# Transposing keys and outputs of a chunked RWKV-7 scan in TensorE's transpose mode

## The chip, the cores and the metric

The kernel runs on one core of one Trainium2 chip, in float32 throughout. The metric is the device time of one execution in microseconds (us). In the profile PE is TensorE's matmul, PEld its weight load, DVE VectorE, ACT ScalarE, POOL GpSimd, SP SyncE, whose queue (SPq) issues most of the DMAs.

## The reference

An encoder of two layers reads 1280 tokens of 1024 channels (a prompt of 256 and a sample of 1024). Layer 0 mixes tokens with a bidirectional RWKV-7 recurrence over 16 heads of 64 channels, layer 1 with neighbourhood attention; each is followed by a squared-ReLU MLP. The change lies in the recurrence alone:

```python
def _wkv_scan(r, w, k, v, a, b, reverse):
    def step(S, inp):
        r_t, w_t, k_t, v_t, a_t, b_t = inp
        sa = jnp.einsum('bhvk,bhk->bhv', S, a_t)
        S = S * w_t[:, :, None, :] + sa[..., None] * b_t[:, :, None, :] + v_t[..., None] * k_t[:, :, None, :]
        return S, jnp.einsum('bhvk,bhk->bhv', S, r_t)
    ...
    _, y = lax.scan(step, s0, seq, reverse=reverse)

# in the mixer: both directions, then a group norm per head, gains, and the bonus
for d in range(2):
    ...
    y = y + _wkv_scan(rf, _heads(decay), k_d, vf, -kk, kk * iclr, reverse=(d == 1))
mu = jnp.mean(y, axis=-1, keepdims=True)
var = jnp.mean(jnp.square(y - mu), axis=-1, keepdims=True)
y = ((y - mu) * lax.rsqrt(var + GN_EPS)).reshape(B, T, C) * lnx_g + lnx_b
y = y + (bonus * vf).reshape(B, T, C)
```

## The kernel before, in words

The scan works on chunks of 64 tokens (`L = 64`), so that the recurrence becomes small matrix products. A job (`scan_job`) takes 16 chunks of one pair of heads: the first head of the pair lies in partitions 0 to 63, the second in 64 to 127. Ten jobs follow each other, and each runs both directions, `d` = 0 forwards and 1 backwards. Within a job the chunks come in groups of four, so there are eight (direction, group) pairs to a job, 80 in all.

The helper `pair` (L995) issues one 64x64 product for each head, one instruction with rows and columns 0 to 63, one with 64 to 127 (or crossed, for the outputs `yo` and `zps`). Every such float32 matmul shows as two records in the trace.

For each (direction, group) pair the program does, among others:

- `prod` (tile `aps`) and `kprod` (tile `kps`): products of keys with queries, masked by DVE into `zb` and `zk`;
- `merge1`, `merge2` (tiles `yps`, `qps`): the second half of an inverse `Q` that DVE and the DMA queues prepare for the next job (`q`, `qt`, `qd`, then `qq` and `qx`);
- `ktr` (L950 to L959), once for each of its four chunks: the keys of both kinds, `bk`, are transposed by multiplying with an identity (tile `lps`, one PSUM bank for both heads), and after the fourth chunk ACT copies the bank to `lt`.

The steps of the recurrence (`scan_step`) use these. A step takes the state `S` through `w` (copied by ACT to `up`), through the inverse (copied to `u`), and through `lt` to the next `S` (ACT again, L1041); its output goes to `yo`. PE, ACT and DVE run in the order in which the program states the work, and that order comes from a time which each piece is given by hand (`at`), so the pieces of `ktr` stand between the steps of the two directions. DMAs on SP's queue are placed by the scheduler.

Four PSUM banks (tag `aps`) go round among the tiles `aps`, `yps`, `kps`, `qps`, `lps` and `zps`. After a job `scan_post` normalises its output `y` in two halves of eight chunks; `tr` (L1114 to L1122) transposes each half, again by products with an identity (tile `zps`), ACT copies it to `zt`, and SP's queue stores it to `z_d`.

Of the kernel before, what the change touches and what calls it, by code (L numbers as in the profile page):

```python
# [5 lines left out]
F32 = mybir.dt.float32  # L6
F32R = mybir.dt.float32r
AF = mybir.ActivationFunctionType
ALU = mybir.AluOpType
# [4 lines left out]
P = 128  # L14
# [4 lines left out]
L = 64  # L19
# [32 lines left out]
class Trunk:  # L52
# [733 lines left out]
    def at(self, t, f, level=3):  # L786
        self.todo.append((t, len(self.todo), f, level))
# [6 lines left out]
    def scan_job(self, j):  # L794
        nc = self.nc
# [3 lines left out]
        J = {"ar": {}, "zb": {}, "zk": {}, "lt": {}}  # L799
# [12 lines left out]
        for n, (d, g) in enumerate(order):  # L812
            m, c0 = grp[g]
            t = T0 + 2 * n if j != 1 or n < 4 else -16.1 + 0.45 * (n - 4)
# [99 lines left out]
        for n, (d, g) in enumerate(order):  # L914
            m, c0 = grp[g]

            def merge1(d=d, g=g):
                zb, qx, lo = J["zb"][d, g], J["qx"][d], 32 * d
                yps = self.pt.tile([P, 4, 32], F32, name="yps", tag="aps")
                for c in range(4):  # L920
                    self.pair(lambda e, z: (yps[z, c, :], zb[z, c, 0:64], qx[z, 4 * g + c, :]))
                yt = J["yt", d, g] = self.nxt(self.r_yt[d])
                nc.scalar.copy(yt[:, :, lo:lo + 32], yps)

            def merge2(d=d, g=g):
                Q, yt, hi = J["Q"], J["yt", d, g], 32 - 32 * d
                qps = self.pt.tile([P, 4, 32], F32, name="qps", tag="aps")
                for c in range(4):
                    self.pair(lambda e, z: (qps[z, c, :], yt[z, c, :], Q[z, 4 * g + c, d, hi:hi + 32]))
                nc.scalar.copy(Q[:, 4 * g:4 * g + 4, d, hi:hi + 32], qps)  # L930
            t = 2 * n - 3.992
            at(t + 0.52, merge1)
            at(t + 1.30, merge2)

            def kload(d=d, g=g, m=m, c0=c0):
                bk = J["bk", d, g] = self.rp.tile([P, 4, P], F32, name="bk", tag="bk", bufs=3)
                nc.sync.dma_start(bk, self.bk_d[m, d, :, c0:c0 + 4, :])

            def kprod(c, d=d, g=g):
                bk, ar = J["bk", d, g], J["ar"][d, g]  # L940
                if c == 0:
                    J["pk"] = self.pa.tile([P, 4, P], F32, name="kps", tag="aps")
                ps = J["pk"]
                self.pair(lambda e, z: (ps[z, c, :], bk[z, c, 64:128], ar[z, c, :]))

            def kmask(d=d, g=g, ps=None):
                zk = J["zk"][d, g] = self.rp.tile([P, 4, P], F32, name="zk", tag="zk", bufs=3)
                nc.vector.tensor_tensor(out=zk, in0=J["pk"], in1=self.mask[d].unsqueeze(1).to_broadcast([P, 4, P]), op=ALU.mult)

            def ktr(c, d=d, g=g):  # L950
                bk = J["bk", d, g]
                if c == 0:
                    J["pl"] = self.pt.tile([P, 4, 2, L], F32, name="lps", tag="aps")
                ps = J["pl"]
                for i in range(2):
                    self.pair(lambda e, z: (ps[z, c, i, :], bk[z, c, 64 * i:64 * i + 64], self.ident[z, z]))
                if c == 3:
                    lt = J["lt"][d, g] = self.rp.tile([P, 4, 2, L], F32, name="lt", tag="lt", bufs=3)
                    nc.scalar.copy(lt, ps)  # L959
            at(t - 1.9 if j or n > 1 else -19.0 + 0.1 * n, kload)  # L960
            at(t + 1.25, kmask)
            for c in range(4):
                at(t + c * 0.11 + 0.80, lambda c=c, f=kprod: f(c))
                at(t + c * 0.11 + 1.53, lambda c=c, f=ktr: f(c))
# [17 lines left out]
        st = [{"S": None}, {"S": None}]  # L982
        for d in range(2):
            for i in range(16):
                cc = i if d == 0 else 15 - i
                m, c0 = grp[cc // 4]
# [13 lines left out]
    def scan_step(self, at, t, J, st, d, cc, m, ch, new, end, i, last):  # L1000
        nc = self.nc
        g, c = cc // 4, cc % 4
        R = {}
        w, us, sn = (lambda s=s: self.pbank[d][:, s] for s in (slice(0, L), slice(L, 2 * L), slice(2 * L, 3 * L)))
        yb = lambda: self.ybank[i // 4 % 2]
        yo = lambda: yb()[:, int(g > 1), c, :]
        half = self.half

        def s0():
            zk, vt = J["zk"][d, g], J["vt"]  # L1010
            self.pair(lambda e, z: (w()[z], zk[z, c, 0:64], vt[z, 0, cc, :]))

        def s1():
            ar, zk, vt = J["ar"][d, g], J["zk"][d, g], J["vt"]
            S = R["S"] = None if new else st["S"]
            if S is not None:
                self.pair(lambda e, z: (w()[z], ar[z, c, 0:64], S[z]), start=False, free=True)
            up = R["up"] = self.sp.tile([P, L], F32, name="up", tag="up", bufs=4)
            nc.scalar.copy(up, w())
            self.pair(lambda e, z: (yo()[half(1 - e)], zk[z, c, 64:128], vt[z, 0, cc, :]), start=d == 0 and i % 4 == 0, free=True)  # L1020

        def s2():
            Q, up, S, ar, vt = J["Q"], R["up"], R["S"], J["ar"][d, g], J["vt"]
            if S is not None:
                self.pair(lambda e, z: (yo()[half(1 - e)], ar[z, c, 64:128], S[z]), start=False, free=True)
            if not end:
                lt = J["lt"][d, g]
                self.pair(lambda e, z: (sn()[z], lt[z, c, 1, :], vt[z, 0, cc, :]), start=False, free=True)
                if S is not None:
                    self.pair(lambda e, z: (sn()[z], self.ident[z, z], S[z]), start=False, free=True)  # L1030
            self.pair(lambda e, z: (us()[z], Q[z, cc, d, :], up[z]), start=last, free=True)
            u = R["u"] = self.sp.tile([P, L], F32, name="u", tag="u", bufs=4)
            nc.scalar.copy(u, us())

        def s3():
            u, zb, y = R["u"], J["zb"][d, g], J["y"]
            if not end:
                lt = J["lt"][d, g]
                self.pair(lambda e, z: (sn()[z], lt[z, c, 0, :], u[z]), start=False, free=True)
                S2 = self.sp.tile([P, L], F32, name="S", tag="S", bufs=5)  # L1040
                nc.scalar.activation(S2, sn(), AF.Copy, scale=self.dall[:, m, d, ch:ch + 1])  # L1041
                st["S"] = S2
            self.pair(lambda e, z: (yo()[half(1 - e)], zb[z, c, 64:128], u[z]), start=False, free=True)
            if d == 1 and i % 4 == 3:
                lo = min(g, 3 - g)
                y = y.rearrange("p (x c) v -> p x c v", c=4)[:, lo:4 - lo:3 - 2 * lo]
                if i < 8:
                    nc.vector.tensor_copy(y, yb())
                else:
                    nc.vector.tensor_tensor(out=y, in0=yb(), in1=y, op=ALU.add)  # L1050
        at(t - 0.68, s0)
        at(t, s1)
        at(t + 0.33, s2)
        at(t + 0.66, s3)

    def scan_post(self, at, J, grp, last):

        nc = self.nc
        for half in range(2):
            st = {}  # L1060
# [3 lines left out]
            t0 = (12.5, 17.496)[half]  # L1064
# [27 lines left out]
            def p3a(st=st, runs=runs):  # L1092
                st["vb"] = self.yp.tile([P, 8, L], F32, name="vb", tag="vb", bufs=2)
                for x, m, c0, g in runs:
                    nc.vector.tensor_tensor(out=st["vb"][:, 4 * x:4 * x + 4], in0=J["vt"][:, 1, 4 * g:4 * g + 4],
                                            in1=self.bonus[:, c0:c0 + 4, m:m + 1].to_broadcast([P, 4, L]), op=ALU.mult)

            def p3b(st=st, runs=runs):
                for x, m, c0, g in runs:
# [12 lines left out]
                eng.tensor_tensor(out=yv(), in0=yv(), in1=st["vb"].rearrange("p (x c) v -> p x c v", c=4), op=ALU.add)  # L1112

            def tr(runs=runs):  # L1114
                ps = self.pt.tile([P, 8, L], F32, name="zps", tag="aps")
                for x, m, c0, g in runs:
                    for c in range(4):
                        self.pair(lambda e, z: (ps[self.half(1 - e), 4 * x + c, :], J["y"][z, 4 * g + c, :], self.ident[z, z]))
                zt = self.yp.tile([P, 8, L], F32, name="zt", tag="zt", bufs=1)
                nc.scalar.copy(zt, ps)  # L1120
                for x, m, c0, g in runs:
                    nc.sync.dma_start(self.scr["z_d"][m, :, c0 * L:(c0 + 4) * L], zt[:, 4 * x:4 * x + 4].rearrange("p c t -> p (c t)"))  # L1122
            for dt, f in ((-0.186, p1), (0.474, p2), (-2.0 - 3.5 * half if last else 1.327, p3a), (1.601, p2b), (-1.9 - 3.5 * half if last else 1.982, p3b), (1.843, p2c), (2.252, p3),
                          (3.521, p4), (4.15, p4b), (4.563, p5), ((6.25, 5.809 if last else 7.25)[half], tr)):
                at(t0 + dt, f)
# [966 lines left out]
```

## Time and profile before

| | |
|---|---|
| median of 3 runs | 3987.63 us (3979.55 to 3991.28) |
| the profiled execution | 3978.29 us, of which its span 3976.5 |
| PE busy | 3742.6 us (94% of the span) |
| DVE, ACT, POOL busy | 2371.8, 1686.8, 1686.1 us |
| the scan, 690 to 1370 us of the span | PE busy 577.24 of 680 us, DVE 374.38, ACT 377.45, POOL 153.85 |
| records of the key transposes (`lps<-cst,bk`) and of the output transposes (`zps<-cst,y`) | 2560 and 640 |
| ACT's copies of them (L959, L1120) | 80 and 20 |

A record's duration on PE is its way through the array; records overlap, so what one costs the engine is the distance between starts, not its duration. In the timeline, rows of the same kind that follow closely are merged (x8), and the second column runs from the first start to the last end.

### The profile page before, as it was taken

What the parts mean: (1) busy time and instruction counts of PE and PEld (TensorE: products, weight loads), DVE (VectorE), ACT (ScalarE), POOL (GpSimd) and SP (SyncE); (2) the same over time, 40 slices, a digit from 0 to 9 for tenths busy, and PEclk for the clock granted to TensorE, in tenths of its full rate; (3) what the DMA queues carried; (4) which work ended last, traced back from release to release, by engine and by line L of the source; (5) the groups of instructions that cost most, each with busy time, mean ns of one, the idle gap of its engine ahead of it and who ended that gap; (6) DMA issues with size and microseconds to landing.
All of it is one profiled execution on the core that took longest, in us unless ns stands there. A gap on an engine that the chain in (4) does not pass through costs nothing.

```text
span 3976.5 us, 89848 instructions
## 1 busy us (share of the span) xinstructions
PE 3742.6 (94%) x36484; PEld 3151.9 (79%) x36484; DVE 2371.8 (60%) x4441; ACT 1686.8 (42%) x4128; POOL 1686.1 (42%) x1540
## 2 busy tenths in 40 slices
PE   8988988888888899999999999999989999999999
PEld 5764578787878787888888889887778788888888
DVE  5778743556565446666666682355563656666666
ACT  6776652555555532222222242466563222222222
POOL 4446552112121334555555551244442445555554
PEclk9997899999999899999999999999999999999999
DMA  4226564767664341111111115444555111111111
GB/s 139 73 100 224 200 227 127 180 164 166 150 165 112 117 131 38 40 38 38 43 43 41 39 61 165 112 109 100 114 135 188 48 35 43 40 43 38 41 40 64
DMA packets 460094, 394.83 MB, mean 99 GB/s; under 512 B 268480, under 2 KB 353856, under 8 KB 459680
## 3 DMA queue, kind: packets, MB, share of 16 engines
q1 hardware_dynamic: 425264, 327.73, 29.8%
q10 hardware_dynamic: 34416, 61.35, 4.2%
q8 instruction: 288, 4.72, 0.5%
q14 instruction: 126, 1.03, 0.1%
HBM read 270.50 MB, written 124.44 MB: 99 GB/s over the span
## 4 chain that ended last, share of the span: by engine, by line
PE 73%; DVE 8%; DMA 7%; ACT 5%; issue 4%; POOL 2%; SPq 1%; ACTq 0%; DVEq 0%; POOLq 0%
PE ps L96 13%; PE ps L97 13%; PE ps L98 12%; PE ps L1480 4%; PE ps L1481 4%; PE ps L1482 4%; PE wu L998 4%; PE vps L513 1%; PE aps L998 1%; PE vps L514 1%; PE vps L515 1%; PE kps L998 1%; DVE q L875 1%; PE op L2004 1%; DMA raw<-in_w_no_dram 1%
## 5 line engine op out<-in xcount | busy, mean ns | idle before, releaser
L96 PE MATMUL ps<-ah,whi 128*128 128x512 f32 (+1 forms) x2304 | 842.8, 366 | 3.9 <-ACT whi L90 3.2
L98 PE MATMUL ps<-ah,wlo 128*128 128x512 f32 (+1 forms) x2304 | 825.3, 358 | 3.2 <-POOL wlo L91 2.7
L97 PE MATMUL ps<-al,whi 128*128 128x512 f32 (+1 forms) x2304 | 826.5, 359 | 0.0
L96 PEld LDWEIGHTS ps<-ah,whi 128*128 128x128 f32 x2304 | 435.0, 189 | 78.6 <-issue 9.0
L98 PEld LDWEIGHTS ps<-ah,wlo 128*128 128x128 f32 x2304 | 434.1, 188 | 76.3 <-DVE wlo L91 4.3
L97 PEld LDWEIGHTS ps<-al,whi 128*128 128x128 f32 x2304 | 435.3, 189 | 65.8 <-issue 1.0
L1484 DVE TENSOR_TENSOR x<-ps,x 128x512 f32<-128x512 f32 x784 | 484.9, 679 | 0.0
L1388 POOL TENSOR_TENSOR rl<-rl 128x512 f32<-128x512 f32 (+1 forms) x192 | 173.6, 904 | 631.1 <-ACT rl L1387 352.4
L1387 ACT ACTIVATE rl<-ps 128x512 f32<-128x512 f32 (+1 forms) x192 | 101.1, 526 | 793.1 <-PE ps L98 793.1
L91 POOL TENSOR_TENSOR wlo<-raw,whi 128x1024 fp32r<-128x1024 f32 (+1 forms) x114 | 235.0, 2061 | 215.7 <-ACT whi L90 189.5
L1480 PE MATMUL ps<-hhTrue,dh 128*128 128x512 f32 x784 | 307.4, 392 | 1.8 <-DVE x L1484 1.8
L1481 PE MATMUL ps<-hlTrue,dh 128*128 128x512 f32 x784 | 307.3, 392 | 0.0
L1482 PE MATMUL ps<-hhTrue,dl 128*128 128x512 f32 x784 | 306.8, 391 | 0.5 <-POOL dl L1372 0.5
L1372 DVE TENSOR_TENSOR hlTrue<-ts,hhTrue 128x512 fp32r<-128x512 f32 x112 | 132.9, 1187 | 150.3 <-ACT hhTrue L1371 150.3
L1372 POOL TENSOR_TENSOR dl<-raw,dh 128x512 fp32r<-128x512 f32 x128 | 208.7, 1643 | 9.4 <-ACT dh L1371 8.4
L90 ACT CAST whi<-raw 128x1024 fp32r<-128x1024 f32 (+1 forms) x142 | 133.3, 939 | 183.4 <-PE ps L97 80.3
L1495 DVE TENSOR_TENSOR x<-ps,x 128x512 f32<-128x512 f32 x224 | 148.8, 686 | 95.1 <-PE ps L98 93.8
L1372 DVE TENSOR_TENSOR hlTrue<-rl,hhTrue 128x512 fp32r<-128x512 f32 x98 | 88.8, 909 | 185.0 <-ACT hhTrue L1371 184.7
L1371 ACT CAST dh<-ds 128x512 fp32r<-128x512 f32 x112 | 69.5, 620 | 278.3 <-POOL ds L1435 278.3
L1372 POOL TENSOR_TENSOR dl<-ds,dh 128x512 fp32r<-128x512 f32 x112 | 158.9, 1419 | 63.5 <-ACT dh L1371 63.5
L1941 POOL TENSOR_TENSOR s<-s,mx 128x384 f32<-128x384 f32 (+1 forms) x150 | 109.9, 745 | 163.9 <-DVE mx L1940 118.3
L1482 PEld LDWEIGHTS ps<-hhTrue,dl 128*128 128x128 f32 x784 | 147.2, 188 | 33.7 <-POOL dl L1372 1.4
(339 smaller groups left out, 10283.4 us busy)
## 6 DMA issues: line engine op xcount, KB each, us to landing
raw<-in_w_down_dram SPq DMA_DIRECT2D x128, 256.0 KB, 2.7
raw<-in_w_up_dram SPq DMA_DIRECT2D x64, 512.0 KB, 3.3
ar<-ar_d SPq DMA_DIRECT2D x80, 256.0 KB, 4.2
bk<-bk_d SPq DMA_DIRECT2D x80, 256.0 KB, 3.6
ar_d<-ar ACTq DMA_DIRECT2D x32, 512.0 KB, 3.1
bk_d<-bk ACTq DMA_DIRECT2D x32, 512.0 KB, 4.0
bs<-tab SPq DMA_DIRECT2D x128, 96.0 KB, 4.1
v_d<-vt ACTq DMA_DIRECT2D x80, 128.0 KB, 3.0
```

The lines of the kernel that those rows point to most:

```text
L91: lo_eng.tensor_tensor(out=lo[:, cs], in0=raw, in1=hi[:, cs].bitcast(F32), op=ALU.subtract)
L96: mm(ps, sh, mh, start=first, stop=False)
L97: mm(ps, sh, ml, start=False, stop=False)
L98: mm(ps, sl, mh, start=False, stop=last)
L998: self.nc.tensor.matmul(out, w, x, start=start, stop=stop, skip_group_check=free)
L1372: eng.tensor_tensor(out=lo, in0=src, in1=hi.bitcast(F32), op=ALU.subtract)
L1388: nc.gpsimd.tensor_tensor(out=r, in0=r, in1=r, op=ALU.mult)
L1480: mm(ch[j], hi[:, cs], hh, start=bool(new), stop=False, skip_group_check=True)
L1481: mm(ch[j], hi[:, cs], hl, start=False, stop=False, skip_group_check=True)
L1482: mm(ch[j], lo[:, cs], hh, start=False, stop=True, skip_group_check=True)
L1484: nc.vector.tensor_tensor(out=xv, in0=ch[j], in1=xv, op=ALU.add)
L1495: nc.vector.tensor_tensor(out=xv, in0=ps, in1=xv, op=ALU.add)
```

## The change

The keys: `ktr` asks for a transpose in place of the product with an identity. Each head has a bank of its own, and both results lie in partitions 0 to 63 of their banks. ACT copies the first head's bank to `lt`, DVE the second's, from partitions 0 to 63 to 64 to 127.

The outputs: `tr` transposes two chunks of both heads as one 128x128 block, four transposes for a half in place of 16 products. The blocks come out with chunk and head in another arrangement, so the chunks 1 and 2 of a group change places in `yo` and in the bonus tile `vb`, ACT's copy to `zt` permutes, and SP stores each half with eight DMAs of 64 partitions in place of two of 128.

```diff
             def ktr(c, d=d, g=g):
                 bk = J["bk", d, g]
                 if c == 0:
-                    J["pl"] = self.pt.tile([P, 4, 2, L], F32, name="lps", tag="aps")
-                ps = J["pl"]
+                    J["pl"] = [self.pt.tile([P, 4, 2, L], F32, name="lps", tag="aps")[0:64] for _ in range(2)]
                 for i in range(2):
-                    self.pair(lambda e, z: (ps[z, c, i, :], bk[z, c, 64 * i:64 * i + 64], self.ident[z, z]))
+                    for e, ps in enumerate(J["pl"]):
+                        z = self.half(e)
+                        nc.tensor.transpose(ps[:, c, i, :], bk[z, c, 64 * i:64 * i + 64], self.ident[z, z])
                 if c == 3:
                     lt = J["lt"][d, g] = self.rp.tile([P, 4, 2, L], F32, name="lt", tag="lt", bufs=3)
-                    nc.scalar.copy(lt, ps)
+                    nc.scalar.copy(lt[0:64], J["pl"][0])
+                    nc.vector.tensor_copy(lt[64:128], J["pl"][1])
...
-        yo = lambda: yb()[:, int(g > 1), c, :]
+        yo = lambda: yb()[:, int(g > 1), (0, 2, 1, 3)[c], :]
...
             def tr(runs=runs):
-                ps = self.pt.tile([P, 8, L], F32, name="zps", tag="aps")
+                ps = self.pt.tile([P, 2, 2, 2, L], F32, name="zps", tag="aps")
                 for x, m, c0, g in runs:
-                    for c in range(4):
-                        self.pair(lambda e, z: (ps[self.half(1 - e), 4 * x + c, :], J["y"][z, 4 * g + c, :], self.ident[z, z]))
-                zt = self.yp.tile([P, 8, L], F32, name="zt", tag="zt", bufs=1)
-                nc.scalar.copy(zt, ps)
+                    for b in range(2):
+                        o = 4 * g + 2 * b
+                        nc.tensor.transpose(ps[:, x, b].rearrange("p e t -> p (e t)"), J["y"][:, o:o + 2, :].rearrange("p a v -> p (a v)"), self.ident)
+                zt = self.yp.tile([P, 2, 2, 2, L], F32, name="zt", tag="zt", bufs=1)
+                nc.scalar.copy(zt, ps.rearrange("p x b e t -> p x e b t"))
                 for x, m, c0, g in runs:
-                    nc.sync.dma_start(self.scr["z_d"][m, :, c0 * L:(c0 + 4) * L], zt[:, 4 * x:4 * x + 4].rearrange("p c t -> p (c t)"))
+                    for i in range(2):
+                        for e in range(2):
+                            t0 = (c0 + 2 * i) * L
+                            nc.sync.dma_start(self.scr["z_d"][m, self.half(1 - e), t0:t0 + 2 * L], zt[self.half(i), x, e].rearrange("p b t -> p (b t)"))
```

PE, in the middle of a job, around one `ktr` (wu, yo: the steps of the two directions), before:

```order
L998 MATMUL wu_7265<-S,ar_6178 64x64 x2
L998 MATMUL yo_7267<-v_7232,zk 64x64 x2
L998 MATMUL lps<-cst,bk 64x64 x8
L998 MATMUL wu_7264<-u,lt 64x64 x2
L998 MATMUL yo_7267<-u,zb_6189 64x64 x2
L998 MATMUL lps<-cst,bk 64x64 x4
L998 MATMUL wu_7265<-v_7232,zk 64x64 x2
```

and after the change:

```order
L1000 MATMUL wu_7265<-S,ar_6178 64x64 x2
L1000 MATMUL yo_7267<-v_7232,zk 64x64 x2
L957 MATMUL lps<-cst,bk 64x64 x8
L1000 MATMUL wu_7264<-u,lt 64x64 x2
L1000 MATMUL yo_7267<-u,zb_6189 64x64 x2
L957 MATMUL lps<-cst,bk 64x64 x4
L1000 MATMUL wu_7265<-v_7232,zk 64x64 x2
```

Nothing moves on PE: the transposes stand where the products stood, in the same 237 stretches between other work (157 of four instructions, 78 of eight, one of 12 and one of 16). The output transposes stand in 19 stretches as before, each of 16 products then and of 4 transposes now (one of 32 and 8).

DVE, in the same job, before (tmp and q: the preparation of the next job's inverse):

```order
L873 TENSOR_TENSOR tmp<-mt,q 128x255
L875 TENSOR_TENSOR q<-q,tmp 128x17x15
L1048 COPY y<-yo_7266 128x2x256
L873 TENSOR_TENSOR tmp<-mt,q 128x256
L875 TENSOR_TENSOR q<-q,tmp 128x16x16
```

and after the change:

```order
L873 TENSOR_TENSOR tmp<-mt,q 128x255
L875 TENSOR_TENSOR q<-q,tmp 128x17x15
L961 COPY lt<-lps 64x512
L1050 COPY y<-yo_7266 128x2x256
L873 TENSOR_TENSOR tmp<-mt,q 128x256
L875 TENSOR_TENSOR q<-q,tmp 128x16x16
```

Each of the 80 new copies stands ahead of work that did not wait for the key transposes before.

SP's queue, at the store of a job's second half, before (qd, qq, qx: the inverse on its way through DRAM to the next job):

```order
L1122 DMA z_d<-zt 128x256 x2
L886 DMA qd<-q 128x1024
L890 DMA qd<-qt 128x1024
L906 DMA qq_7234<-qd 32x16x32 x4
L911 DMA qx_7268<-qd 32x16x32 x2
L906 DMA qq_7234<-qd 32x16x32 x4
L911 DMA qx_7277<-qd 32x16x32 x2
L838 DMA dd<-zb_7246 128x4x64
L937 DMA bk<-bk_d 128x512
```

and after the change:

```order
L1129 DMA z_d<-zt 64x128 x8
L886 DMA qd<-q 128x1024
L890 DMA qd<-qt 128x1024
L937 DMA bk<-bk_d 128x512
L906 DMA qq_7234<-qd 32x16x32 x4
L911 DMA qx_7268<-qd 32x16x32 x2
L906 DMA qq_7234<-qd 32x16x32 x4
L911 DMA qx_7277<-qd 32x16x32 x2
L838 DMA dd<-zb_7246 128x4x64
```

Eight stores stand ahead of the inverse's store where two stood, and one load of keys has come ahead of the inverse's twelve loads.

More of the change, by code (lines that the diff above doesn't have):

```diff
@@ L1094, in p3a @@
                 for x, m, c0, g in runs:
-                    nc.vector.tensor_tensor(out=st["vb"][:, 4 * x:4 * x + 4], in0=J["vt"][:, 1, 4 * g:4 * g + 4],
-                                            in1=self.bonus[:, c0:c0 + 4, m:m + 1].to_broadcast([P, 4, L]), op=ALU.mult)
+                    nc.vector.tensor_tensor(out=st["vb"][:, 4 * x:4 * x + 4].rearrange("p (b a) v -> p b a v", b=2),
+                                            in0=J["vt"][:, 1, 4 * g:4 * g + 4].rearrange("p (a b) v -> p b a v", a=2),
+                                            in1=self.bonus[:, c0:c0 + 4, m:m + 1].rearrange("p (a b) o -> p b a o", a=2).to_broadcast([P, 2, 2, L]), op=ALU.mult)
             def p3b(st=st, runs=runs):
```

## The prediction

> **What bounds the kernel now.** I read the page first, then the scan stretch by stretch, the chain of waits there, the groups by line and what PE waits for, and last the timeline of PE around single transposes. The change touches only the scan, 690 to 1370 us. One row of busy times by stretch, the shares of the chain of waits from 935 to 975 us, and two rows of the groups by line:
>
> ```profile
> 690.00:1370.00 680.00, 577.24 (x18822) 536.66 (x18819) 374.38 (x936) 377.45 (x1399) 153.85 (x174) 0.95 0.60 148
> by line: PE wu L998 30.4%; issue 13.8%; PE aps L998 7.3%; PE lps L998 7.1%; PE kps L998 6.3%; PE yps L998 6.2%; PE yo L998 5.7%; ACT mt L862 5.7%; PE qps L998 3.1%; ACT qt L888 3.1%; ACT S L1041 2.1%; PE zps L998 2.1%; ACT up L1019 1.9%; AC
> L998 PE MATMUL lps<-cst,bk 64*64 64x64 f32 x2542 | 120.3, 222 | 5.4 <-issue 4.5 <-PE wu L998 0.6
> L998 PE MATMUL zps<-cst,y 64*64 64x64 f32 x640 | 25.0, 228 | 10.4 <-DVE y L1112 8.0 <-issue 2.4
> ```
>
> PE is busy 577 of 680 us, DVE 374 and ACT 377, and the chain of waits goes through PE's small products: PE's order of work sets the scan's end. So a microsecond put on PE or taken off counts, unless it falls into one of PE's waits. These are the waits that ACT ends (PE's rows by wait; total, times, longest):
>
> ```profile
> PE wu L998 <- ACT up L1019: 15.9, 28, 4.9
> PE yo L998 <- ACT u L1033: 10.4, 12, 1.0
> PE wu L998 <- ACT u L1033: 6.1, 14, 1.4
> PE wu L998 <- ACT S L1041: 5.9, 7, 2.1
> ```
>
> They are 38.3 us in 61 waits. A transpose can hide only in these, and only where the ACT copy does not itself come behind the transpose.
>
> **What a product costs now.** PE's timeline in the middle of a job:
>
> ```profile
> 946.58 0.28 PE L998 MATMUL wu<-up,qq 64*64 64x64 f32 x4
> 946.70 0.40 PE L998 MATMUL lps<-cst,bk 64*64 64x64 f32 x8
> 946.93 0.28 PE L998 MATMUL aps<-ar,bb 64*64 64x128 f32 x2
> ```
>
> Eight records take 0.23 us from start to start; the two heads run together, so a pair of records costs 0.058 us. The keys have 2560 records, 1280 pairs: 74 us. The outputs have 640, 320 pairs: 18.6 us.
>
> **What a transpose costs.** The attention layer has 128x128 float32 transposes (L1947), here between dense products of a steady 0.12 us:
>
> ```profile
> 2599.86 0.28 PE L98 MATMUL ps<-ah,wlo 128*128 128x256 f32 x1
> 2599.98 0.49 PE L1947 MATMUL pt<-cst,s 128*128 128x128 f32 x3
> 2600.23 0.36 PE L96 MATMUL ps<-ah,whi 128*128 128x256 f32 x1
> 2600.43 0.28 PE L97 MATMUL ps<-al,whi 128*128 128x256 f32 x1
> ```
>
> Three transposes and one product take 2600.43 - 2599.98 = 0.45 us; less 0.12 that is 0.11 a transpose, with one record each where a float32 product has two. So the outputs need 80 x 0.11 = 8.8 us. A 64x64 transpose is not in this trace. With half the columns it lies between 0.055 (half of 0.11) and 0.058 (a pair's records now); I take 0.058. If the two heads run together, 640 pairs cost 37 us; if not, 74. For the first speaks that two row halves of the array do run together in another stage, over all 128 columns and into two banks:
>
> ```profile
> 478.51 0.40 PE L97 MATMUL rps<-ml,wh 128*128 128x512 f32 x1
> 478.75 0.39 PE L98 MATMUL rps<-mh,wl 128*128 128x512 f32 x1
> 479.06 0.48 PE L599 MATMUL ltw<-tw,wa 64*128 64x256 f32 x1
> 479.07 0.48 PE L599 MATMUL lta<-ta,wa 64*128 64x256 f32 x1
> 479.38 0.38 PE L599 MATMUL ltw<-tw,wa 64*128 64x256 f32 x1
> ```
>
> **What changing the array's layout costs.** Today every product of the scan's middle is 64*64 (the row's first pair of numbers: rows and columns that it uses). The 128x128 transposes are not, and the two heads' 64x64 transposes now write the same partitions of two banks, which no pair of 64*64 products here does. What a change of layout costs stands before the scan, where `prod` alternates with dense products:
>
> ```profile
> 618.72 0.28 PE L514 MATMUL vps<-wl,mh 128*128 128x256 f32 x1
> 618.84 0.28 PE L515 MATMUL vps<-wh,ml 128*128 128x256 f32 x1
> 619.04 1.09 PE L998 MATMUL aps<-ar,bb 64*64 64x128 f32 x16
> 620.07 0.39 PE L513 MATMUL vps<-wh,mh 128*128 128x256 f32 x1
> 620.29 0.28 PE L514 MATMUL vps<-wl,mh 128*128 128x256 f32 x1
> ```
>
> Dense products follow at 0.12. The first 64*64 product comes 0.20 after the last dense one: 0.08 lost. Its eight pairs follow at (1.09 - 0.28) / 7 = 0.116, so the next dense product was due at 619.97 and came at 620.07: 0.10. The one after was due at 620.19 and came at 620.29, its weights not loaded ahead: 0.10 again. A round trip costs 0.28 us. The change to 64*128 above costs the same kind: 478.75 to 479.06 is 0.31, where the dense product before it took 0.24.
>
> For the keys the price of a round trip lies between 0 (the 64x64 transposes stay in the layout) and 0.28; I take 0.28, because every change of layout seen here pays it, and because of the shared output partitions. The Trainium skill, "TensorEngine Tiling (Array Packing)", says in Tiling Modes that a change of mode drains the engine, and under Restrictions that column tiling switches the transpose mode off for fp32 input. By these each stretch of key transposes must leave the 64*64 layout; the 0.08 and 0.10 agree with the first, and no row here can show the second.
>
> **The sum on PE.** Keys: 237 stretches x 0.28 = 66 us, plus 37, less 74: +29 us. Outputs: 19 x 0.28 = 5.3, plus 8.8, less 18.6: -4.5 us. Together +24.5. The same order stays between the stretches, so nothing else moves on PE.
>
> **What hides of it.** A stretch of two pairs grows from 0.23 to 0.40 us, by 0.16; one of four pairs from 0.46 to 0.51, by 0.05. At most 61 waits x 0.16 = 10 us can take this up. Not all lie behind a transpose, and ACT's 0.59 us copy of the keys stands in ACT's queue ahead of the next `up`, so that a later transpose makes a later step. Between 0 and 10 I take 7.
>
> **The other engines.** Copies from PSUM, by groups:
>
> ```profile
> L959 ACT COPY lt<-lps 128x512 f32<-128x512 f32 x80 | 47.1, 589 | 4.3 <-PE lps L998 4.1
> L888 ACT COPY qt<-q 128x256 f32<-128x256 f32 x36 | 23.0, 641 | 6.3 <-DVE q L875 6.3
> L862 ACT COPY mt<-mraw 64x256 f32<-64x256 f32 x36 | 22.7, 632 | 7.3 <-DMA mraw<-dd 6.7
> L1048 DVE COPY y<-yo 128x512 f32<-128x512 f32 x20 | 13.7, 683 | 6.8 <-PE yo L998 6.4 <-PE wu L998 0.2
> ```
>
> L888 and L862 differ by half the partitions and hardly in time, so ACT's key copy stays at 0.59 us and ACT gains nothing. DVE gets 80 copies of about 0.68 us, 54 us on top of 374: it still idles a third of the time, which hides them. The four waits on ACT above are long, and PE waits for DVE only at the last job's outputs (the 8.0 us in the row of zps). Behind a copy on DVE queue the updates of the next inverse and the masks that free banks; ACT waited 6.3 us for the inverse (L888's row), and with six tiles going round four banks where five did, a mask that is late now holds PE. I give DVE and banks 0 to 6 us and take 1. If DVE had no idle time, its copies would cost up to 54. The swapped chunks in `yo` and `vb` and the permuting copy to `zt` move as many elements in runs of 64 as before: nothing, and if the 20 copies to `zt` took twice their time, 12 us on ACT, which idles 300.
>
> On SP's queue, the stores' own row, the stretch that follows one of them, and the waits in it:
>
> ```profile
> L1122 SPq DMA_DIRECT2D z_d<-zt x40: 319/422/1659, 785.3 to 1369.4; - x40
> 942.49 1.22 SPq L1122 DMA_DIRECT2D z_d<-zt  x2
> 944.25 0.32 SPq L886 DMA_DIRECT2D qd<-q  x1
> 947.43 0.32 SPq L890 DMA_DIRECT2D qd<-qt  x1
> SPq L890 <- ACT u L1033: 17.7, 8, 2.9
> PE yps L998 <- DMA qx<-qd: 6.2, 2, 5.3
> PE aps L998 <- DMA ar<-ar_d: 6.3, 5, 2.4
> ```
>
> Six more stores of 0.42 us are 2.5 us, 20 times. Behind the second half's stores wait qd and the loads of qq and qx, for which PE's `yps` waits; but L890 idles 17.7 us in 8 jobs, 2.2 each, so of 2.5 us 0.3 is left, and about a store's 0.4 for the load of keys that now comes first. Behind the first half's stand loads of `ar`, which PE already meets late five times. If nothing covered them, 20 x 2.5 = 50 us; with the cover I take 2 of the range 0 to 10.
>
> The forecast: +24.5 - 7 + 1 + 2 = +20 us. The profiled execution of 3978.3 (span 3976.5 and 1.8 around it) would become 3998. It lies 9.3 below the median of the runs, 3987.6, so the median would be **4008 us**.
>
> **Rivals.**
>
> *The transposes stay cheap.* If the key transposes keep to the 64*64 layout, or the array need not empty for them, PE saves 37 us on the keys and, without any price for layouts, 9.8 on the outputs: -47. Waits that ACT ends grow where PE comes sooner; with the same 10 us lost to them -37, and +3 for DVE and SP: -34, 3954 us. It decides from the round trip's price: 47 us over 256 stretches is 0.18 us; below that PE gains, above it PE loses. For it: one record in place of two, and no 64-row transpose in the trace to contradict. Against: the 0.28 of 618 to 620 us. The Trainium skill, "Perfetto Trace Analysis", section Optimizing Tensor Performance, wants logical transposes done as transposes and not as products; by it this rival would be the forecast, and the rows of L1947 agree as to one record each.
>
> *The heads run one after the other*, or each transpose still takes two passes: 37 us more, +57, 4045 us. Against it the 0.01 us between L599's rows; for it that these are no transposes.
>
> *The waits take it.* PE's loss is real, but falls into idle time to the full 10 us, and a round trip costs less than 0.28: 0.10 of it was a load of 128 columns of weights, and 64 columns may take half. 256 x 0.23 = 59, less 47, less 10 and plus 3 is +5 us, 3993. For it PE's 103 us without work; against it that only 61 waits have the right releaser.
>
> **How the numbers follow.** Chances: forecast 0.50 (its own range 3998 to 4025), cheap transposes 0.18, heads in turn 0.12, waits 0.20. A difference under 0.3%, 12 us, cannot be told from none here. Slower: 0.47 of the forecast, 0.12, and 0.02 of the waits, 0.61. Faster: 0.17 of the first rival and no other. The rest, 0.22, is no difference. The range 3964 to 4044 leaves out most of the first rival's lower half and the upper half of the second's.
>
> **What would show it.** In the profile after: 1280 records of `lps<-cst,bk`, 80 of `zps`; pairs of heads starting within 0.01 us (else the second rival); about 0.14 us lost before the first transpose of a stretch and again behind the last (if the products follow at 0.06 without a gap, the first rival). A stretch of eight transposes lasts 0.5 us with its gaps, one of four 0.4. ACT's key copy stays at 0.59, DVE's new one is near 0.68. I am wrong in kind if the scan is shorter, or if PE's waits on DVE or on qx grow by more than 10 us.

## The result, and the profile after

The changed kernel takes 4017.07 us (median of 4 runs, 4009.39 to 4022.47), the kernel before in the same runs 3983.59 (3976.53 to 3991.28). The ratio is 1.0079, with a 95% interval of 1.0058 to 1.0101: 31 us slower by the ratio, 33.5 by these medians, where the prediction said 20. Below, differences in microseconds are the ratio to the kernel before times its median. Three later executions that took 4925, 12468 and 16914 us, two of experiments and one of the kernel before, are left out of the ratios as slow ones.

The profile after is of an execution of 4014.23 us with a span of 4012.4, 35.9 more than before. Nearly all of it lies inside the scan: its last store to `z_d` starts at 1403.3 us, where it started at 1369.4. The rows of the two stores, of the key transposes and their two copies, and of the output transposes, by tile (line, engine, operation, tile, count; shortest, median and longest in ns; first and last start):

```profile
L1129 SPq DMA_DIRECT2D z_d<-zt x160: 446/595/1697, 790.0 to 1403.3; - x160
L957 PE MATMUL lps<-cst,bk x1280: 213/216/313, 691.1 to 1375.6; 64*64 64x64 f32 x183
L960 ACT COPY lt<-lps x80: 577/579/600, 692.1 to 1375.9; 64x512 f32<-64x512 f32 x80
L961 DVE COPY lt<-lps x80: 683/684/685, 692.2 to 1376.0; 64x512 f32<-64x512 f32 x80
L1122 PE MATMUL zps<-cst,y x80: 272/273/448, 788.2 to 1397.6; 128*128 128x128 f32 x80
```

The counts and copies are as forecast: 1280 and 80 records, 0.58 us on ACT, 0.68 on DVE. PE's timeline shows a stretch with one chunk's four transposes in the middle of a job:

```profile
956.36 0.23 PE L1000 MATMUL yo<-u,zb 64*64 64x64 f32 x2
956.52 0.30 PE L957 MATMUL lps<-cst,bk 64*64 64x64 f32 x4
956.88 0.27 PE L1000 MATMUL wu<-v,zk 64*64 64x64 f32 x2
956.90 0.27 PE L1000 MATMUL yo<-S,ar 64*64 64x64 f32 x2
956.99 0.23 PE L1000 MATMUL wu<-v,zk 64*64 64x64 f32 x2
```

The first transpose comes 0.15 us after the last product's second record, where 0.06 is normal. In a trace of single records the two heads' transposes start 0.003 us apart, the first pair takes 0.082 and later ones 0.056; the product behind the last comes 0.146 later, and the next one 0.11 behind that in place of 0.06. (These are medians over the stretches at full clock. In the stretch shown the product behind comes 0.28 later, because it also waits for ACT's `up`.) So a round trip costs 0.09 + 0.025 + 0.09 + 0.05, about 0.25 us, and the stretches pay it although their records still show 64*64.

And yet the experiments below show that PE's added work is hardly where the time went. PE's waits of the kernel after (total, times, longest; a selection):

```profile
PE wu L1000 <- ACT u L1035: 15.9, 21, 2.1
PE yps L1000 <- DMA qx<-qd: 12.6, 10, 3.9
PE wu L1000 <- ACT up L1021: 12.0, 21, 4.8
PE wu L1000 <- DVE zk L948: 6.7, 9, 1.5
PE wu L1000 <- DVE tmp L873: 2.0, 1, 2.0
PE aps L1000 <- DVE lt L961: 1.7, 1, 1.7
PE wu L1000 <- issue: 4.9, 7, 1.8
```

The waits for qx doubled, from 6.2 us in two to 12.6 in ten; waits for DVE's `zk`, `tmp` and `lt` came up, which were 0.8 us before. In exchange, waits on nothing that the profile shows (issue) shrank, from 32.6 us in all to 9.7. The waits for `u` ahead of `wu` grew most, from 6.1 to 15.9 us, but they are 12.2 in `e6_outs_poolq` too, which loses nothing. All of PE's waits from 690 to 1410 us sum to 99 us before and after, so this sum alone does not say whether PE's added work or work that came late elsewhere made the scan longer. SP's queue in the same job, where before two stores took 1.22 us ahead of qd:

```profile
952.56 6.24 SPq L1129 DMA_DIRECT2D z_d<-zt  x8
958.91 0.52 SPq L886 DMA_DIRECT2D qd<-q  x1
959.52 0.38 SPq L890 DMA_DIRECT2D qd<-qt  x1
959.99 0.74 SPq L937 DMA_DIRECT2D bk<-bk_d  x1
```

That points at two terms that the prediction held small (SP's queue 2 us, DVE 1) rather than at its large one (PE 24.5). The experiments take them apart.

### The profile page after: what moved, and what is told of

The parts are those of the page before. It is cut to its first block, busy times and chain, and to the rows that moved or that the text cites. A ratio compares the mean times of both kernels' runs of the same rounds, so it can differ in the third digit from the quotient of the medians.

```text
span 4012.4 us, 86430 instructions
## 1 busy us (share of the span) xinstructions
PE 3775.2 (94%) x34644; PEld 3150.1 (79%) x34644; DVE 2423.8 (60%) x4521; ACT 1686.8 (42%) x4128; POOL 1685.5 (42%) x1540
## 4 chain that ended last, share of the span: by engine, by line
PE 72%; DVE 8%; DMA 6%; ACT 5%; issue 3%; POOL 3%; SPq 2%; ACTq 0%; DVEq 0%; POOLq 0%
PE ps L96 13%; PE ps L97 13%; PE ps L98 13%; PE ps L1487 4%; PE ps L1488 4%; PE ps L1489 4%; PE wu L1000 3%; DVE q L875 1%; PE vps L513 1%; PE vps L514 1%; PE vps L515 1%; PE aps L1000 1%; DVE tmp L873 1%; PE op L2011 1%; DMA raw<-in_w_no_dram 1%
## 5 line engine op out<-in xcount | busy, mean ns | idle before, releaser
L1081 POOL TENSOR_TENSOR y<-y,mu 128x512 f32<-128x512 f32 x18 | 19.2, 1067 | 374.1 <-DVE mu L1078 345.6
```

## The experiments

### The two halves apart, and the key transposes in one stretch

`e1_keys` takes only `ktr` of the change, `e2_outs` only the outputs' part (`yo`, `p3a`, `tr`). `e3_group` is the whole change with the four calls of `ktr` at one place, `e4_group_prod` the kernel before with the same move:

```
-                at(t + c * 0.11 + 1.53, lambda c=c, f=ktr: f(c))
+                at(t + 1.86, lambda c=c, f=ktr: f(c))
```

> Only the keys' half of the change; the outputs stay products. Theory (every stretch of key transposes pays a round trip of the array's layout, 237 of them at 0.26 to 0.28 us): +24 to +34 us against the kernel before, about all of the +33 of the whole change. Rival (most of the +33 comes from the outputs' eight stores on SP's queue and the late loads of qx behind them): +12 to +20 us.

> Only the outputs' half: y transposed two chunks and heads at once, eight stores of each half; the keys stay products. Theory: PE saves 4 to 5 us, SP's queue takes 0 to 8 and the last stores come some 4 us later: -4 to +8 us against the kernel before. Rival (the stores are the main loss): +12 to +20 us.

> The whole change, but the 16 key transposes of a (d, g) stand in one stretch, so 80 stretches in place of 237. Theory (round trips are the price): 157 x 0.26 us = 41 us less on PE than the whole change, of which perhaps 10 come back as waits: -30 to -41 us against the change, -8 to +3 us against the kernel before. Rival (the price lies in the copies, the banks and the stores, which stay as they are): within 8 us of the change, +25 us or more against the kernel before.

> The kernel before, with the key products of a (d, g) in one stretch too; nothing is transposed. It prices the new order alone. Theory: no layout changes here, so nothing but the order moves: within 6 us of the kernel before, a little slower if anything, since 0.9 us of products now stands in front of a step at once. Rival (a better order is what makes the grouped transposes fast): -15 us or more.

Measured, ratio to the kernel before: keys alone 1.0040 (1.0025 to 1.0056), +16 us; outputs alone 1.0053 (1.0036 to 1.0069), +21; grouped 1.0098 (1.0080 to 1.0115), +39; grouped products 1.0052 (1.0034 to 1.0070), +21. The outputs, expected between a gain of 4 us and a loss of 8, lose as much as the keys or more. `e1_keys` lies in the range of its rival, `e2_outs` just above its own, and `e4_group_prod` outside both of its expectations. And grouping the transposes, which saves 157 round trips and so some 40 us of PE's time, gains nothing. A part of that is the order: a stretch of 0.9 us at once stands ahead of a step of the scan, and PE then waits more for the step's copies. PE's waits of `e4_group_prod`, which were 15.9, 6.1 and 10.4 us before:

```profile
PE wu L998 <- ACT up L1019: 22.9, 38, 5.1
PE wu L998 <- ACT u L1033: 20.1, 67, 0.9
PE yo L998 <- ACT u L1033: 14.5, 17, 1.5
```

With the order at 21, grouping should still leave 20 us of PE's 41 as a gain over the whole change; it has +39 where that has +31. Either the order costs more with transposes, or PE's time does not come out as the kernel's time.

### The outputs: it is the stores

In `e2_outs` SP's queue shows eight stores where two were, and PE's wait for qx is 20.2 us. SP's timeline in the middle of a job, and the row of PE's waits:

```profile
948.71 5.58 SPq L1127 DMA_DIRECT2D z_d<-zt  x8
954.40 0.52 SPq L886 DMA_DIRECT2D qd<-q  x1
```

```profile
PE yps L998 <- DMA qx<-qd: 20.2, 12, 6.0
```

Three kernels test it. `e5_stores8` cuts the stores of the kernel before into eight and changes nothing else:

```
-                    nc.sync.dma_start(self.scr["z_d"][m, :, c0 * L:(c0 + 4) * L], zt[:, 4 * x:4 * x + 4]...)
+                    for i in range(2):
+                        for e in range(2):
+                            t0, k = (c0 + 2 * i) * L, 4 * x + 2 * i
+                            nc.sync.dma_start(self.scr["z_d"][m, self.half(e), t0:t0 + 2 * L], zt[self.half(e), k:k + 2]...)
```

`e6_outs_poolq` is the outputs' half with the stores on another queue, `e8_outs_4st` with four stores in place of eight:

```
-                            nc.sync.dma_start(self.scr["z_d"][m, self.half(1 - e), t0:t0 + 2 * L], ...)
+                            nc.gpsimd.dma_start(self.scr["z_d"][m, self.half(1 - e), t0:t0 + 2 * L], ...)
```

```
-                nc.scalar.copy(zt, ps.rearrange("p x b e t -> p x e b t"))
+                nc.scalar.copy(zt, ps.rearrange("p x b e t -> p x e b t")[:, :, ::-1])
...
+                        nc.sync.dma_start(self.scr["z_d"][m, :, t0:t0 + 2 * L].rearrange("(e v) t -> v e t", e=2),
+                                          zt[self.half(i), x].rearrange("p e b t -> p e (b t)"))
```

> The kernel before, in which only the two stores of each half's outputs are cut into the eight of the change (64 rows by two chunks each); every product, copy and tile stays. Theory (the eight stores hold SP's queue for 5.6 us instead of 1.2 ahead of qd and the loads of qq and qx, and the next job's merges wait): +12 to +22 us against the kernel before, with PE's wait for qx above 15 us. Rival (the outputs' loss lies in the 128x128 transposes, their banks or the copy to zt): within 5 us of the kernel before.

> The outputs' half of the change alone, its eight stores issued from POOL's queue instead of SP's. Theory (SP's queue is the whole loss of this half): PE's 4 to 5 us saved come out, -6 to +3 us against the kernel before; PE's wait for qx back to about 6 us. Rival (the loss stays with the transposes or the copy): +12 to +20 us. A third way: POOL's own work comes late behind the issue of its stores, +5 to +12.

> The outputs' half alone with four stores on SP's queue in place of eight, each for both heads (the ACT copy swaps the heads in zt, so that one store can take both). Theory (SP's queue, price by the number of stores): four take about 2.6 us, 1.4 more than before, so a third of the loss: 0 to +8 us against the kernel before. Rival (the price goes by bytes and rows, not by the number of stores): +14 to +20 us as with eight.

Measured: eight stores in the kernel before 1.0101 (1.0082 to 1.0119), +40 us; the outputs' half with its stores on POOL's queue 1.0002 (0.9991 to 1.0013); with four stores 0.9995 (0.9981 to 1.0009). PE's wait for qx with eight stores in the kernel before:

```profile
PE yps L998 <- DMA qx<-qd: 19.1, 12, 4.3
```

The same wait with four stores of the transposed outputs, and behind it the row of these stores by tile:

```profile
PE yps L998 <- DMA qx<-qd: 9.1, 5, 6.4
```

```profile
L1126 SPq DMA_DIRECT2D z_d<-zt x80: 575/602/2654, 788.4 to 1385.0; - x80
```

So the outputs' loss is their stores in SP's queue: the stores alone bring it without a transpose, and it goes with another queue (the wait is 6.9 us there) or with half the stores. A store of 64 rows by 128 numbers takes 0.595 us, one of twice as many 0.602, and the old one of four times as many 0.422, so the price does not go by bytes but with the number of stores. One thing more goes with it. In the four kernels with eight stores on SP's queue the scheduler also put a load ahead of the inverse's twelve loads in seven or eight jobs, nearly always one of keys, as in the change. It holds the queue for 0.4 to 0.7 us, in four cases for 2.0 to 2.5. With four stores one job or none has it. So the number of stores and the order that came with it were not separated. That 40 us came where the whole half loses 21 was not expected: the profiles show 35 windows at half clock where `e2_outs` has 29 (see the last section), up to 10 us by an estimate, and the rest of the excess is open. A gain of 4.5 us on PE is not to be seen in either mended kernel; only the interval of the one with four stores would hold it.

### The keys: it is not the transposes

`e7_keys_dve` is the kernel before, its bank copied half by ACT and half by DVE. `e9_two_banks` is the keys' half in all but the transposes: banks, copies and DVE's order of the change, the products of before.

```
-                    nc.scalar.copy(lt, ps)
+                    nc.scalar.copy(lt[0:64], ps[0:64])
+                    nc.vector.tensor_copy(lt[64:128], ps[64:128])
```

```
-                    J["pl"] = self.pt.tile([P, 4, 2, L], F32, name="lps", tag="aps")
+                    J["pl"] = [self.pt.tile([P, 4, 2, L], F32, name="lps", tag="aps") for _ in range(2)]
...
-                    self.pair(lambda e, z: (ps[z, c, i, :], bk[z, c, 64 * i:64 * i + 64], self.ident[z, z]))
+                    self.pair(lambda e, z: (J["pl"][e][z, c, i, :], bk[z, c, 64 * i:64 * i + 64], self.ident[z, z]))
...
-                    nc.scalar.copy(lt, ps)
+                    nc.scalar.copy(lt[0:64], J["pl"][0][0:64])
+                    nc.vector.tensor_copy(lt[64:128], J["pl"][1][64:128])
```

> The kernel before, with the copy of the keys split: ACT copies the lower 64 partitions, DVE the upper 64 of the same bank; the products stay, nothing is transposed. It prices DVE's new copy and the mask zk behind it. Theory (the keys' +15 us are PE's round trips): 0 to +5 us against the kernel before. Rival (DVE's copy in its in-order queue is the keys' loss): +10 to +16 us.

> The keys' half of the change without its transposes: the two heads write banks of their own and ACT copies one, DVE the other, all in the change's order, but each head is multiplied by the identity as in the kernel before. So PE's products and layout are those of before, while banks, copies and DVE's queue are those of the change. Theory A (the keys' +15 us are PE's round trips of the layout): -2 to +5 us against the kernel before. Theory B (they are DVE's copy, behind which zk and the inverse are late): +10 to +16 us.

Measured: 1.0030 (1.0018 to 1.0041), +12 us, and 1.0034 (1.0019 to 1.0050), +14 us, where the keys' half with its transposes had +16. The products in place of the transposes change nothing that can be told: the second theory holds, and the round trips are not the keys' loss. In the waits of `e9_two_banks` those of DVE for the keys' products, of ACT for the last update of the inverse (6.3 us before), and of PE for DVE and for nothing shown:

```profile
DVE lt L959 <- PE lps L998: 74.4, 37, 7.9
ACT qt L888 <- DVE q L875: 11.3, 9, 4.3
PE wu L998 <- DVE zk L948: 4.5, 6, 1.5
PE wu L998 <- issue: 7.1, 14, 1.2
PE yo L998 <- issue: 6.7, 11, 1.3
```

DVE's work stays in its order. The copy stands among the inverse's updates, or waits for PE with masks behind it. DVE's timeline of the changed kernel shows one among updates that otherwise follow each other without a gap:

```profile
942.22 0.42 DVE L875 TENSOR_TENSOR q<-q,tmp 128x247 f32<-128x247 f32 x1
942.67 0.68 DVE L961 COPY lt<-lps 64x512 f32<-64x512 f32 x1
943.39 0.41 DVE L873 TENSOR_TENSOR tmp<-mt,q 128x240 f32<-128x240 f32 x1
```

In a usual job five copies lie between the inverse's first update and its last, and this stretch takes 40.3 us in `e9_two_banks`, 39.8 in the change and 39.0 before (medians of six jobs). The stretch is a sign and not a measure of the loss, though: of the two kernels at the end of the next section, `e11_after4` has the five copies and 39.1 us, `e12_after4_act` no copy on DVE and 40.4. `e7_keys_dve` has DVE's copy and no second bank, so a second bank is not needed for the loss; there DVE's copy waits for ACT's, though (112.4 us in 45 waits), so it is a harder case. So DVE's copy is shown as the cause; how the loss divides between a late inverse and late masks was not separated.

### What PE's round trips cost, and both copies on ACT

`e10_extra_trips` puts 160 round trips into the kernel before, each one 128x128 transpose into the bank ahead of the products that overwrite it:

```
+                if c % 2 == 0:
+                    nc.tensor.transpose(ps[:, c].rearrange("p i t -> p (i t)"), bk[:, c, :], self.ident)
```

> The kernel before with 160 added round trips and nothing else: for two of the four chunks of a (d, g) one 128x128 transpose is put into the bank ahead of the key products, which overwrite it. By the prediction's prices a trip is 0.28 us and the transpose 0.11: 62 us on PE. If PE's order sets the scan's end and its waits hide 10 to 12 us, as the prediction had it: +45 to +55 us against the kernel before. Rival (PE has more cover than that, so a round trip in the middle of the scan costs much less than 0.28): +10 to +35 us.

Measured: 1.0038 (1.0024 to 1.0053), +15 us. PE's timeline at one of them:

```profile
948.24 0.23 PE L1000 MATMUL wu<-S,ar 64*64 64x64 f32 x2
948.40 0.33 PE L956 MATMUL lps<-cst,bk 128*128 128x128 f32 x1
948.66 0.62 PE L1000 MATMUL lps<-cst,bk 64*64 64x64 f32 x14
```

The products were due at 948.30 and come at 948.66: 0.36 for the trip and the transpose, close to the 0.39 of the prediction's prices. 160 of them are 57 us on PE, of which 15 come out (10 to 21 by the interval). The waits took in about 31: all of PE's waits from 690 to 1410 us sum to 99 us before and to 68 here, `up` 15.9 to 11.2, `u` 16.5 to 5.5, issue 32.6 to 19.9.

```profile
PE wu L1000 <- ACT up L1021: 11.2, 19, 3.9
PE yo L1000 <- ACT u L1035: 4.1, 8, 0.6
PE wu L1000 <- ACT u L1035: 1.4, 7, 0.3
PE wu L1000 <- issue: 8.0, 11, 1.2
```

That leaves 26 us. The spans of the two profiled executions differ by 24 (4000.7 and 3976.5), more than the 15 of the ratio, since the one of the kernel before is 9 us faster than the median of its runs. The keys' half repeats it: the same sum is 109 us in `e9_two_banks` and 87 in `e1_keys`, 22 less, about what the transposes add on PE (237 x 0.25, plus 36, less 74: 21). The ratios of the two leave room for a part of it: they differ by 2 us, with up to some 11 inside their intervals.

Last, two kernels of the whole change: `e11_after4` with four stores as above, `e12_after4_act` with four stores and this:

```
-                    nc.vector.tensor_copy(lt[64:128], J["pl"][1])
+                    nc.scalar.copy(lt[64:128], J["pl"][1])
```

> The whole change with four stores of each half's outputs in place of eight (the ACT copy swaps the heads in zt). If the stores are the outputs' whole loss and the two halves add: the keys' +15 remain, +11 to +19 us against the kernel before, 15 to 22 less than the change. Rival (with the keys slower, qx is late anyway and the stores matter less): +22 to +32 us.

> The whole change with four stores of the outputs and with both copies of the keys on ACT, so that DVE has the work of the kernel before. If DVE's copy is the keys' loss because it stands among the updates of the inverse, and ACT's 46 us more lie in its idle time: -10 to +2 us against the kernel before, faster than the variant with four stores and DVE's copy (+5). Rival (ACT sits on the chain of u, up and S, and a second copy of 0.58 us in its queue is as late for them as DVE's is for the inverse): +8 to +25 us.

Measured: 1.0012 (1.0001 to 1.0023), +5 us, and 1.0063 (1.0041 to 1.0085), +25 us. The first lies below both of its expectations, the second in its rival's. Four stores take 27 of the change's 31 us away, more than the stores' part should be if the halves added (keys +16, outputs with four stores -2); that gap stays open. So the halves do not add: the keys' half costs 16 us alone, some 10 on top of eight stores and 7 on top of four. Nor do the waits for DVE price it, for `e11_after4` still has 14.3 us of ACT waiting for the inverse and 5.3 of PE waiting for `zk`. On ACT the second copy is dearer than on DVE. DVE is then relieved (ACT waits 5.0 us for the inverse, PE 0.4 for `zk`), but PE waits for `up`, 12.0 us with DVE's copy:

```profile
PE wu L1000 <- ACT up L1021: 52.7, 70, 5.0
ACT qt L888 <- DVE q L875: 5.0, 8, 0.7
PE wu L1000 <- DVE zk L948: 0.4, 1, 0.4
```

No variant beats the kernel before by more than its runs can tell.

| kernel | ratio to before | us |
|---|---|---|
| the change | 1.0079 | +31 |
| the change, four stores | 1.0012 | +5 |
| the change, four stores, both copies on ACT | 1.0063 | +25 |
| keys' half | 1.0040 | +16 |
| keys' half, products in place of transposes | 1.0034 | +14 |
| outputs' half | 1.0053 | +21 |
| outputs' half, four stores / POOL's queue | 0.9995 / 1.0002 | -2 / +1 |
| before, eight stores | 1.0101 | +40 |
| before, 160 more round trips | 1.0038 | +15 |
| before, DVE copies half of the keys | 1.0030 | +12 |
| the change, key transposes grouped / before, key products grouped | 1.0098 / 1.0052 | +39 / +21 |

## Why the prediction was right or wrong

The direction and roughly the time were right, for the wrong reason: the large term is nearly nothing, and two small ones are the loss. That the time came near is luck: PE's net 17.5 us were too many, and the 3 of DVE and SP's queue too few.

- **The price of a round trip, 0.28 us: right.** 0.25 us measured, by the pieces that were named: about 0.09 on each side and weights that are not loaded ahead. The heads run together (0.003 us apart) and a pair takes 0.056, so the second rival is out, and so is the first, in which the transposes stay in the 64*64 layout. The Trainium skill, "TensorEngine Tiling (Array Packing)", Tiling Modes, says that a change of mode drains the engine; the gaps on both sides of the stretch agree.
- **"What hides of it", 7 us of at most 10: wrong, and this is the step that failed.** It took only the 61 waits that ACT ends, and in each only one stretch's growth. The 32.6 us of issue in the waits were left out, and the chain "PE's order of work sets the scan's end" was read from busy shares and from the chain's shares in 40 us. `e10_extra_trips` shows 57 us put on PE and 15 come out; `e9_two_banks` against `e1_keys` shows that of some 21 us on PE for the keys 2 come out, 11 at most. The third rival had this mechanism, though with a smaller share.
- **SP's queue, 2 us of 0 to 10: mis-sized tenfold.** The mechanism was there, in the right place: stores ahead of qd, with the loads of qx behind and `yps` waiting. The price of a store was the median of larger stores, 0.42 us; eight of the new ones hold the queue for 5.5 to 6.2 us in the change where two took 1.22. With 4.4 us more and the same cover of 2.2 for each job, the prediction's own step gives 2.2 us in each of the eight jobs in which stores stand ahead of qd, some 18 in all. That is an estimate made afterwards, near the 21 of the outputs' half; the same stores in the kernel before cost 40, so it is not confirmed. The load of keys that comes first was priced at 0.4 us and took 0.7.
- **DVE and banks, 1 us of 0 to 6: mis-sized.** `e9_two_banks` measures 14, though on top of four stores the keys' half costs 7. "It still idles a third of the time, which hides them" is an average; the copies stand in the inverse, whose updates follow each other almost without a gap, and ahead of masks.
- **ACT gains nothing from half the partitions: right,** 0.579 us against 0.589.
- By its own mark the prediction is wrong in kind: PE's waits on DVE (`zk`, `tmp`, `lt` and a `zb` of 1.0) grew from 0.8 us to some 12, above the 10 that it named.

## What to carry to other kernels

Count the instructions that a changed layout of the output puts on a DMA queue, and price them by the stretch of the queue in which they stand, not by a median of other transfers: here they cost at least as much as the whole half of the keys. A busy share over a whole stage hides nothing by itself; an added instruction costs what the work behind it in its engine's order loses, and here that was the inverse or the masks on DVE and `up` on ACT. Halves of a change that meet in the same waits need not add. That an engine is 85% busy with its lines on the chain of waits does not make its microseconds the kernel's; an added dummy load on it tells, and it took one run.

## What the runs showed of the hardware

The granted clock of TensorE goes down after a window in which PE idles for a part only. Averaged over the timed runs it is 0.970 for the kernel before, 0.964 for the change, 0.966 for the keys' half, 0.968 for the same with products, and 0.972 for the kernel with 160 more round trips, which is slower and yet clocked higher. Windows of 3.41 us in the changed kernel show how (busy us and records of PE, PEld, DVE, ACT and POOL, then PE's clock, the DMA share and GB/s):

```profile
951.33:954.75 3.42, 3.42 (x108) 3.19 (x107) 3.21 (x11) 1.86 (x7) 0.00 (x0) 1.00 0.46 101
954.75:958.16 3.41, 2.01 (x56) 1.47 (x52) 0.76 (x4) 2.87 (x10) 0.00 (x0) 1.00 0.15 31
958.16:961.57 3.41, 3.41 (x77) 3.41 (x74) 0.39 (x1) 1.36 (x6) 0.00 (x0) 0.50 0.64 228
961.57:964.99 3.42, 3.42 (x124) 3.19 (x117) 1.12 (x2) 2.10 (x9) 0.00 (x0) 0.99 0.86 224
```

The window with 56 records is followed by one at half clock. Counted over all fourteen profiles from 690 to 1370 us, a full-clock window with fewer than 44 records was always followed by half clock, one with more than 73 never, and between them both occur. By PE's busy time the bounds are 1.52 and 2.30 of 3.41 us; which of the two counts was not separated. At half clock the products take twice as long: pairs of `kps` records start 0.213 us apart in place of 0.111. To the end of its scan the kernel before has 20 windows at half clock, the change 35, `e1_keys` 35 where `e9_two_banks` with products has 28, and `e5_stores8`, which has only products, 35 as well. So both the transposes with their gaps and long waits bring them. The Trainium skill, "TensorE: Matmul & The Clock Gate", Part 1, says that the clock falls to half after an idle window of about 3.4 us; here it falls after a window in which PE ran for 2.01 of 3.41 us, so the measurement differs. The 15 windows more at half pace are up to 26 us of PE's work (an estimate: 15 x 3.41, halved), so the clock is a real part of the change's loss. It does not decide it alone: the change with four stores has 35 such windows too, and +5 us. How much of the lost time comes from the clock, and how much of the clock from the lost time, the runs don't separate.

Also not expected: a store of 64 rows by 128 numbers holds SP's queue for 0.595 us, longer than one of 128 rows by 256 (0.422).
